# Normalization of the attention output through the z gates' buffers, its loads begun by ScalarE, and a fixed order up to the third feed-forward pair

## The chip, the cores and the metric

The kernel runs on one core of one Trainium2 chip. The metric is device time in microseconds (us) of one execution. Names of engines are those of the profile: PE is TensorE's matmul, DVE is VectorE, ACT is ScalarE, POOL is GpSimd, SP is SyncE, which here only issues transfers (its queue is SPq in the profile). ACT issues transfers too, in order with its other instructions.

## The reference

One hybrid decoder layer of width 1024 on 1024 positions, in float32. Cut to what matters:

```python
h = rms_norm(x, norm_mix_g)
z, xbc, dt_raw, q_a, kv_a, k_rope_raw, gates = split(h @ w_in)
y_ssd = ssd_mixer(z, xbc, dt_raw, ...) @ w_ssd_proj
y_mla = mla_mixer(q_a, kv_a, k_rope_raw, ...) @ w_mla_proj
g_ssd, g_mla = split(sigmoid(gates + gate_b), 2)
x = x + (g_ssd * y_ssd + g_mla * y_mla) @ w_o
h = rms_norm(x, norm_ffn_g)
u = causal_depthwise_conv(h @ w_up, conv_ffn_w, conv_ffn_b)      # 3 taps, 2 * 2816 channels
u_gate, u_val = split(u, 2)
x = x + (silu(u_gate) * u_val) @ w_down
```

`ssd_mixer` puts `xbc` through a causal convolution and silu, runs a state-space scan in chunks of 128 positions over 4 groups of 8 heads, multiplies by silu(z) and normalizes by group. `mla_mixer` is causal softmax attention with 16 heads of 64 values.

## The kernel before

**Products.** Every float32 operand of a large product is split into a high and a low part of a reduced float32 type (fp32r): ACT casts the high part (L127), and DVE or POOL subtracts to get the low part (L128). A product is three matmuls for each 128 x 128 x 512 piece (L149, L150, L151: high by high, high by low, low by high). A tile of weights for 128 output rows comes as two raw transfers of 256 KB (`wraw`, L134, two buffers), issued from SP; ACT casts `whi`, and POOL makes `wlo` until the last state-space group, DVE after it. Activations are held split in tiles `h`; `load_act` (L156) and `load_at` (L256) load a raw tile and split it.

**Stages.** In the profile's time: the norm and the small projections until about 100 us; attention until about 706 us, with gate tiles (`gate_tile`) and z tiles (`z_tiles`) as background work on PE; the last of these z tiles until about 750 us; the six tiles of the first convolution group (`conv_group(0)`: the B and C rows of the group, then four x tiles) until about 842 us; state-space groups 0 to 2 until about 1180 us, with the next convolution group and z tiles as background; group 3 with the attention output's projection (`mla_tiles`) in the background until about 1345 us; the projections by `w_ssd` and `w_o`; the seam, in which the first three pairs of feed-forward tiles (`q0`, `q1`, `q2`) begin, until about 1690 us; the steady pairs until about 2050 us; the product by `w_down`.

**What lies in memory between stages.** Attention writes its unnormalized output to `at_d` and 1/l, the reciprocal of each softmax denominator, to `l_d`. `normalize(n)` (L926), called sixteen times from the state-space loop (L874 and what follows), makes it whole: it loads a 128 x 512 piece of `at_d` into a tile `rb` (L934), broadcasts two rows of `l_d` into a second tile `rb` (L936, two transfers), multiplies on POOL (L937), and at the next call stores the piece back (L929). All of it is issued from SP. `load_at` reads the finished pieces, eight in `z_tiles(14, 15)` into tiles `rb` and eight in `mla_tiles` into tiles `lt`. The z tiles go to `z_d`, 256 KB each; `z_load` (L749) brings 256 KB of them per chunk into a tile `zt` (issued from ACT), and DVE uses it at L862. `abc_load` (L741) broadcasts 512 KB per chunk, also from ACT. In `mla_tiles`, `one` (L944) loads a gate tile of `g_d` into a tile `rb` (L947), combines it with the product and stores it to `m_d` (L954).

**What sets the order.** PE's instructions are always in the order of the program. For the other engines a scheduler chooses the order from what each instruction needs, buffers among it: the sixteen normalizations are called once per chunk of groups 0 and 1, but their data is there earlier, and nothing but their buffers holds them. Buffers are taken in turn by name within a pool; the pool `dp` (L734) has two of each name unless `bufs` says otherwise, so before there were three `rb`, shared by both tiles of `normalize`, `load_at` and `one`, and two `zt`. Between `strict` (L1267) and `strict_end` (L1355) each engine except SP keeps the order of the program by added dependencies; this covers part of the seam.

**The feed-forward pairs.** A pair is a gate tile and a value tile of 1024 positions. Each is computed by a scheme of seven products p1 to p7 on sums of blocks of the operands. For one pair: `w_raw` loads, `w_first`, `w_sums`, `w_second`, `w_third`, `w_fourth` make and split the weight sums; `p5`, `p6`, `p7`, `p3`, `p4` are products on PE; `both_sums` (L1221, the sum at L1223) reads the accumulator that `p3` goes on to; `c22` (L1233, the sum at L1235) reads the one that `p4` goes on to; `c11`, `c21` and `p3`'s last line write the other quarters of the rows `ug` and `uv`. `gate` (L1250) convolves `ug` (one ACT step, two DVE steps at L1243) and applies silu; `value` (L1260) convolves `uv`, multiplies with the gate (L1262) and stores.

Of the kernel before, what the change touches and what calls it, by code (L numbers as in the profile page):

```python
# [9 lines left out]
F32 = mybir.dt.float32  # L10
F32R = mybir.dt.float32r
I32 = mybir.dt.int32
AF = mybir.ActivationFunctionType
# [4 lines left out]
P = 128  # L18
# [9 lines left out]
FFT = 22  # L28
# [44 lines left out]
def tile_hybrid_layer(ctx: ExitStack, tc: tile.TileContext, x, cols, cons, w_main, w_small, w_uq, w_ukv,  # L73
# [180 lines left out]
    at = []  # L254

    def load_at(k, s, pool, name):  # L256
        raw = pool.tile([P, 512], F32, name=name, bufs=3)
        nc.sync.dma_start(out=raw, in_=at_d[k * P:(k + 1) * P, s])
        t = act_tile()
        split(raw, t[:, 0, :], t[:, 1, :])  # L260
        return t
# [472 lines left out]
    with tc.tile_pool(name="dp", bufs=2) as dp, tc.tile_pool(name="psx", bufs=1, space=PSUM) as psx, \  # L734
# [14 lines left out]
        def z_load(n):  # L749

            if n < GROUPS * NT:
                g, c = divmod(n, NT)
                t = dp.tile([P, 4, P], F32, name="zt")
                nc.scalar.dma_start(out=t, in_=z_d[4 * g * P:4 * (g + 1) * P, c * P:(c + 1) * P]
                                    .rearrange("(j p) t -> p j t", p=P))
                zts.append(t)
# [169 lines left out]
        def normalize(n):  # L926

            if stores:
                nc.sync.dma_start(out=stores[0][0], in_=stores[0][1])  # L929
                stores.pop()  # L930
            if n < 16:
                k, s = n // 2, hs_(n % 2)
                raw, rb = [dp.tile([P, 512], F32, name="rb", bufs=3) for _ in range(2)]
                nc.sync.dma_start(out=raw, in_=at_d[k * P:(k + 1) * P, s])  # L934
                for hd in range(2):
                    nc.sync.dma_start(out=rb[64 * hd:64 * hd + 64, :], in_=l_d[2 * k + hd, s].partition_broadcast(64))  # L936
                G.tensor_tensor(raw, raw, rb, op=ALU.mult)  # L937
                stores.append((at_d[k * P:(k + 1) * P, s], raw))

        def mla_tiles():  # L940

            at1 = []

            def one(w, ct, half):  # L944
                s = hs_(half)
                gt = dp.tile([P, 512], F32, name="rb", bufs=3)
                nc.sync.dma_start(out=gt, in_=g_d[(8 + ct) * P:(9 + ct) * P, s])  # L947
                ps = lin_tile()
                for k, _ in enumerate(steps([w], (at, at1)[half], ps, range(KD), KD)):
                    if len(at1) < 8 and k % 4 == 0:  # L950
                        at1.append(load_at(len(at1), hs_(1), lt, "lt"))
                    yield True
                V.scalar_tensor_tensor(gt, gt, 1.0, ps, op0=ALU.add, op1=ALU.mult)
                nc.sync.dma_start(out=m_d[ct * P:(ct + 1) * P, s], in_=gt)  # L954

            for ct in range(4):
                yield from one(load_w(w_mla[ct], [P, KD, P]), ct, 0)
            for ct in range(4, 8):
                w = load_w(w_mla[ct], [P, KD, P])
                for half in range(2):  # L960
                    yield from one(w, ct, half)
            for ct in range(4):
                yield from one(load_w(w_mla[ct], [P, KD, P]), ct, 1)
                ya0[ct] = load_act(y_d, ct * P, hs_(0))
# [63 lines left out]
    def w_raw(q):  # L1028
        q.r1 = up.tile([P, KD, P], F32, name="ur1", bufs=2)
        q.r2 = up.tile([P, KD, P], F32, name="ur2", bufs=2)  # L1030
        nc.sync.dma_start(out=q.r1, in_=w_up[q.j])
        nc.sync.dma_start(out=q.r2, in_=w_up[FFT + q.j])
# [14 lines left out]
    def w_first(q):  # L1047
        q.a = w_split(q.r1, w_tiles(0), G)
# [14 lines left out]
    def w_fourth(q, n=3):  # L1063
        q.d = w_split(q.r1[:, 4:8, :], w_tiles(n, n == 1), V)
# [8 lines left out]
    with tc.tile_pool(name="ep", bufs=2) as ep:  # L1073
# [127 lines left out]
        def gate_row(q):  # L1201
            q.ug = up.tile([P, T + 2], F32, name="ug", bufs=2)
            G.memset(q.ug[:, 0:2], 0.0)

        def c11(q):
            s1 = lt.tile([P, 512], F32, name="lt")
            S.copy(s1, q.x)
            V.tensor_tensor(q.ug[:, 2:514], q.y, s1, op=ALU.add)

        def p5(q):  # L1210
            q.z = bank6()
            drain([product(q.z, q.b, 0, "t1", True, True)])
# [16 lines left out]
        def value_row(q):  # L1229
            q.uv = ux[0].tile([P, T + 2], F32, name="uv", bufs=2)  # L1230
            G.memset(q.uv[:, 0:2], 0.0)
# [5 lines left out]
        def conv(q, kind, u):  # L1237
            c = ux[0].tile([P, T], F32, name=f"uc{kind}", bufs=2 - kind)
            ct = kind * FFT + q.j
            cw = CG_FW + 3 * ct  # L1240
            S.activation(c, u[:, 2:T + 2], AF.Identity, bias=col(CG_FB + ct), scale=col(cw + 2))
            for k in range(2):
                V.scalar_tensor_tensor(c, u[:, k:k + T], col(cw + k), c, op0=ALU.mult, op1=ALU.add)  # L1243
            return c

        def p3(q):
            drain([product(q.z, q.d, 0, "22", False, True)])
            V.tensor_tensor(q.ug[:, 514:1026], q.z, q.s2, op=ALU.add)

        def gate(q):  # L1250
            q.gate = conv(q, 0, q.ug)
            S.activation(q.gate, q.gate, AF.Silu)

        def p4(q):
            drain([product(q.y, q.e or q.c, 0 if q.e else 4, "t4", False, True)])
# [1 line left out]
        def c21(q):  # L1257
            V.tensor_tensor(q.uv[:, 2:514], q.y, q.s2, op=ALU.add)  # L1258

        def value(q):  # L1260
            c = conv(q, 1, q.uv)
            V.tensor_tensor(q.gate, q.gate, c, op=ALU.mult)  # L1262
            nc.sync.dma_start(out=a_d[q.j * P:(q.j + 1) * P, :], in_=q.gate)

# [85 lines left out]
    for n, q in enumerate((q0, q1)):  # L1352
        w_fourth(q, 3 if n == 0 else 1)
        p4(q)
    strict_end = len(nc.cur_bb.bb.instructions)  # L1355
    w_raw(q2)
    w_sums(q2)
    for q in (q0, q1):
        value_row(q)
        S.copy(q.uv[:, 514:1026], q.q)  # L1360
        c21(q)
    w_second(q2, V)
    w_third(q2)
    p3(q0)
    gate(q0)
    p3(q1)
    w_fourth(q2)
    q = q2

    rows = "p a b -> p (a b)"  # L1370
# [6 lines left out]
        split(raw, *first[k])  # L1377

    for j in range(3, FFT + 1):
        nx = None  # L1380
        if j < FFT:
            nx = Pair()
            nx.j = j
            w_raw(nx)
            w_first(nx)
        p5(q)
        if j == 3:
            gate_row(q)
            c11(q)
        if nx:  # L1390
            w_sums(nx)
        p6(q)
        if j == 3:

            value(q0)
            gate(q1)
        if nx:
            gate_row(nx)
        if nx:
            w_second(nx)  # L1400
        if not nx:
            for k in range(2):
                first_acts(k)
        p7(q)
        c22(q)
        p3(q)
        if j == 3:
            value(q1)
        gate(q)
        if nx:  # L1410
            w_fourth(nx)
        p4(q)
        c21(q)
        if not nx:
            for k in range(2, 4):
                first_acts(k)
        value(q)
        if nx:
            w_third(nx)
            drain([p12(nx)])  # L1420
            c11(nx)
        q = nx
# [130 lines left out]
```

## Time and profile before

| | us |
|---|---|
| median of 3 executions | 2294.0 |
| their lowest and highest | 2285.99, 2294.86 |
| the profiled execution, whole | 2296.51 |
| its span, first to last instruction | 2294.4 |
| mean granted TensorE clock in it | 0.988 |

Durations come from that one profiled execution. A row of a group names the line, the engine, the operation, what it writes and reads, and how often. In a row of waits, what stands left of the arrow sat idle until what stands right of it was done. A row of windows gives, for a stretch of the span, its length, the busy time of each engine with the number of instructions, the granted TensorE clock as a share of full speed, the share of time in which the transfer engines were busy, and GB/s.

### The profile page before, as it was taken

To read this page: it belongs to the slowest core of one execution; us is meant where nothing else is said; L and a number is where in the kernel's file an instruction comes from. 1 tells how busy PE (TensorE), PEld (TensorE's weight loads), DVE (VectorE), ACT (ScalarE), POOL (GpSimd) and SP (SyncE) were. 2 spreads that over 40 slices of the span, in tenths; PEclk is the share of its full clock that TensorE was granted. 3 is DMA by queue.
4 is the path that set the end of the run, shared out by engine and by line. 5 is a ranking of instruction groups with operands and counts; after the bars stand their busy time and mean duration, and the time that the engine had idled before them with its cause. 6 is when DMAs were issued, how large, how long until landed. Compare 5 with 4: busy or idle time off the path is not lost. (4 is left out here: it accounts for less than half of the span.)

```text
span 2294.4 us, 31427 instructions
## 1 busy us (share of the span) xinstructions
PE 2205.7 (96%) x11488; PEld 1769.3 (77%) x11488; DVE 1430.9 (62%) x2496; ACT 1014.1 (44%) x1852; POOL 755.5 (33%) x821
## 2 busy tenths in 40 slices
PE   8999999999998879999998999999989999999999
PEld 7877777777776667777876778989778888888887
DVE  4566565667662348887876755645887767774432
ACT  5454454454543226565654423424544444443221
POOL 2244432444333444343423310003175555510000
PEclk9999999999999999999999999999999999999999
DMA  3111111111113542545356685543122222227541
GB/s 141 57 66 48 48 42 52 53 48 41 54 48 117 168 147 75 126 104 124 97 156 189 170 280 197 178 144 116 55 92 83 83 83 83 83 101 269 189 148 65
DMA packets 158906, 253.57 MB, mean 111 GB/s; under 512 B 13504, under 2 KB 68480, under 8 KB 158752
## 3 DMA queue, kind: packets, MB, share of 16 engines
q1 hardware_dynamic: 101232, 214.73, 27.2%
q10 hardware_dynamic: 57520, 36.84, 6.8%
q8 instruction: 90, 1.47, 0.3%
q14 instruction: 64, 0.52, 0.1%
HBM read 194.63 MB, written 56.89 MB: 110 GB/s over the span
## 5 line engine op out<-in xcount | busy, mean ns | idle before, releaser
L149 PE MATMUL lin<-h,whi 128*128 128x512 f32 x1440 | 601.1, 417 | 16.4 <-ACT whi L127 10.5
L151 PE MATMUL lin<-h,wlo 128*128 128x512 f32 x1440 | 570.2, 396 | 16.9 <-POOL wlo L128 15.9
L150 PE MATMUL lin<-h,whi 128*128 128x512 f32 x1440 | 568.2, 395 | 0.0
L149 PEld LDWEIGHTS lin<-h,whi 128*128 128x128 f32 x1440 | 274.3, 191 | 124.0 <-issue 57.0
L151 PEld LDWEIGHTS lin<-h,wlo 128*128 128x128 f32 x1440 | 273.5, 190 | 83.6 <-POOL wlo L128 21.3
L150 PEld LDWEIGHTS lin<-h,whi 128*128 128x128 f32 x1440 | 274.7, 191 | 53.7 <-issue 7.3
L127 ACT CAST whi<-wraw 128x512 fp32r<-128x512 f32 x276 | 165.3, 618 | 301.9 <-PE lin L150 118.0
L128 POOL TENSOR_TENSOR wlo<-wraw,whi 128x512 fp32r<-128x512 f32 x134 | 198.8, 1498 | 188.6 <-ACT whi L127 188.5
L621 ACT ACTIVATE e<-s 128x512 f32<-128x512 f32 (+1 forms) x192 | 93.5, 491 | 162.1 <-DVE s L619 111.2
L128 DVE TENSOR_TENSOR wlo<-wraw,whi 128x512 fp32r<-128x512 f32 x142 | 99.7, 721 | 93.2 <-ACT whi L127 93.1
L626 POOL TENSOR_TENSOR acc<-acc,e 128x512 f32<-128x512 f32 (+3 forms) x80 | 79.2, 990 | 224.1 <-ACT acc L624 134.4
L128 DVE TENSOR_TENSOR h<-ar,h 128x1024 fp32r<-128x1024 f32 x40 | 48.7, 1225 | 109.0 <-ACT h L127 108.9
L808 ACT ACTIVATE seg<-abc,acum 128x128 f32<-128x128 f32 x256 | 82.2, 390 | 41.8 <-PE yp L849 35.2
L127 ACT CAST h<-ar 128x1024 fp32r<-128x1024 f32 x40 | 42.0, 1054 | 125.8 <-PE lin L150 115.0
L770 DVE SCALAR_TENSOR_TENSOR xg<-craw,cl,xg 128x1024 f32<-128x1024 f32 x48 | 76.6, 1596 | 33.3 <-ACT xg L768 31.5
L149 PE MATMUL dps<-whi,h 128*128 128x512 f32 x240 | 93.4, 389 | 0.0
L150 PE MATMUL dps<-wlo,h 128*128 128x512 f32 x240 | 93.4, 389 | 0.0
L151 PE MATMUL dps<-whi,h 128*128 128x512 f32 x240 | 93.4, 389 | 0.0
L626 DVE TENSOR_TENSOR acc<-acc,e 128x512 f32<-128x512 f32 (+3 forms) x80 | 58.4, 730 | 48.9 <-ACT e L621 33.2
L632 PE MATMUL pv<-e,vt 128*64 128x512 f32 (+3 forms) x384 | 83.1, 513 | 0.0
L1096 POOL TENSOR_TENSOR h<-x,h 128x512 fp32r<-128x512 f32 x8 | 11.1, 1390 | 214.9 <-ACT h L1095 214.9
L1043 ACT CAST xhi<-ur 128x512 fp32r<-128x512 f32 (+1 forms) x41 | 34.0, 830 | 91.7 <-PE dps L150 86.6
(566 smaller groups left out, 5157.9 us busy)
## 6 DMA issues: line engine op xcount, KB each, us to landing
wraw<-in_w_main SPq DMA_DIRECT2D x112, 256.0 KB
ur<-in_w_up SPq DMA_DIRECT2D x44, 512.0 KB
ar<-a_d SPq DMA_DIRECT2D x40, 512.0 KB
abc<-ac_d ACTq DMA_DIRECT2D x32, 512.0 KB
wraw<-in_w_ssd SPq DMA_DIRECT2D x64, 256.0 KB
wraw<-in_w_down SPq DMA_DIRECT2D x44, 256.0 KB
a_d<-uc SPq DMA_DIRECT2D x22, 512.0 KB
g_d<-lt SPq DMA_DIRECT2D x32, 256.0 KB
```

The costliest lines, as they stand in the source:

```text
L127: S.copy(hi, raw)
L128: (eng or V).tensor_sub(lo, raw, hi.bitcast(F32))
L149: PE.matmul(ps, lhsT=ah, rhs=bh, start=first, stop=False, **more)
L150: PE.matmul(ps, lhsT=ah, rhs=bl, start=False, stop=False, **more)
L151: PE.matmul(ps, lhsT=al, rhs=bh, start=False, stop=last, **more)
L621: S.activation(e[:, c0:512], ps[:, 0:w], AF.Exp)
L626: (V if hd else G).tensor_tensor(accs[hd][:, c0:512], accs[hd][:, c0:512], e[:, c0:512], op=ALU.add)
L632: PE.matmul(pv[hd * 64:(hd + 1) * 64, c0:512], lhsT=vt[:, j, hd * 64:(hd + 1) * 64], rhs=es[hd][:, c0:512], start=first, stop=last)
L770: V.scalar_tensor_tensor(c, raw[:, k:k + T], col(cw + k), c, op0=ALU.mult, op1=ALU.add)
L808: S.activation(seg[:, hd, :], abc[:, hd, :], AF.Relu, bias=acum[:, c, 8 * g + hd:8 * g + hd + 1], scale=-1.0)
L1043: S.copy(hi, r)
L1096: eng.tensor_sub(lo, v, hi.bitcast(F32))
```

## The change

It has four parts.

1. In `normalize` the broadcast of 1/l goes into a tile `zt`, shared with the z gates' loads; `zt` has three buffers instead of two, and `rb` two instead of three. The three `zt` buffers are taken in turn by z loads and broadcasts, so a broadcast waits for the use of an earlier z tile, and a z load for an earlier normalizing product.
2. `load_at` issues its sixteen transfers from ACT instead of SP. Its tiles `rb` have two buffers; `lt` keeps the pool's three.
3. `one` in `mla_tiles` has its gate tiles in two buffers `rb` instead of three.
4. In the seam `gate` and `value` can be called in two parts (convolution; silu or product and store), the fixed order reaches to the second part of `value(q1)`, behind `p3(q2)`, and the steps of the third pair and the beginning of the fourth are written out in it. The loop over pairs then begins with what is left of the third pair.

The diff, cut to its core:

```diff
--- before.py
+++ after.py
@@ -254,8 +254,8 @@
     at = []
     def load_at(k, s, pool, name):
-        raw = pool.tile([P, 512], F32, name=name, bufs=3)
-        nc.sync.dma_start(out=raw, in_=at_d[k * P:(k + 1) * P, s])
+        raw = pool.tile([P, 512], F32, name=name)
+        nc.scalar.dma_start(out=raw, in_=at_d[k * P:(k + 1) * P, s])
         t = act_tile()
         split(raw, t[:, 0, :], t[:, 1, :])
         return t
@@ -750,7 +750,7 @@
             if n < GROUPS * NT:
                 g, c = divmod(n, NT)
-                t = dp.tile([P, 4, P], F32, name="zt")
+                t = dp.tile([P, 4, P], F32, name="zt", bufs=3)
                 nc.scalar.dma_start(out=t, in_=z_d[4 * g * P:4 * (g + 1) * P, c * P:(c + 1) * P]
                                     .rearrange("(j p) t -> p j t", p=P))
                 zts.append(t)
@@ -930,7 +930,9 @@
                 stores.pop()
             if n < 16:
                 k, s = n // 2, hs_(n % 2)
-                raw, rb = [dp.tile([P, 512], F32, name="rb", bufs=3) for _ in range(2)]
+                raw = dp.tile([P, 512], F32, name="rb")
+
+                rb = dp.tile([P, 4, P], F32, name="zt", bufs=3).rearrange("p a b -> p (a b)")
                 nc.sync.dma_start(out=raw, in_=at_d[k * P:(k + 1) * P, s])
                 for hd in range(2):
                     nc.sync.dma_start(out=rb[64 * hd:64 * hd + 64, :], in_=l_d[2 * k + hd, s].partition_broadcast(64))
@@ -943,7 +945,7 @@
             def one(w, ct, half):
                 s = hs_(half)
-                gt = dp.tile([P, 512], F32, name="rb", bufs=3)
+                gt = dp.tile([P, 512], F32, name="rb")
                 nc.sync.dma_start(out=gt, in_=g_d[(8 + ct) * P:(9 + ct) * P, s])
                 ps = lin_tile()
                 for k, _ in enumerate(steps([w], (at, at1)[half], ps, range(KD), KD)):
@@ -1247,9 +1249,11 @@
             drain([product(q.z, q.d, 0, "22", False, True)])
             V.tensor_tensor(q.ug[:, 514:1026], q.z, q.s2, op=ALU.add)
-        def gate(q):
-            q.gate = conv(q, 0, q.ug)
-            S.activation(q.gate, q.gate, AF.Silu)
+        def gate(q, part=None):
+            if part != 1:
+                q.gate = conv(q, 0, q.ug)
+            if part != 0:
+                S.activation(q.gate, q.gate, AF.Silu)
         def p4(q):
             drain([product(q.y, q.e or q.c, 0 if q.e else 4, "t4", False, True)])
@@ -1257,10 +1261,12 @@
         def c21(q):
             V.tensor_tensor(q.uv[:, 2:514], q.y, q.s2, op=ALU.add)
-        def value(q):
-            c = conv(q, 1, q.uv)
-            V.tensor_tensor(q.gate, q.gate, c, op=ALU.mult)
-            nc.sync.dma_start(out=a_d[q.j * P:(q.j + 1) * P, :], in_=q.gate)
+        def value(q, part=None):
+            if part != 1:
+                q.value = conv(q, 1, q.uv)
+            if part != 0:
+                V.tensor_tensor(q.gate, q.gate, q.value, op=ALU.mult)
+                nc.sync.dma_start(out=a_d[q.j * P:(q.j + 1) * P, :], in_=q.gate)
@@ -1352,19 +1358,41 @@
     for n, q in enumerate((q0, q1)):
         w_fourth(q, 3 if n == 0 else 1)
         p4(q)
-    strict_end = len(nc.cur_bb.bb.instructions)
+    for q in (q0, q1):
+        value_row(q)
+    for q in (q0, q1):
+        S.copy(q.uv[:, 514:1026], q.q)
+        c21(q)
     w_raw(q2)
     w_sums(q2)
-    for q in (q0, q1):
-        value_row(q)
-        S.copy(q.uv[:, 514:1026], q.q)
-        c21(q)
+    value(q0, 0)
+    p3(q0)
     w_second(q2, V)
     w_third(q2)
-    p3(q0)
-    gate(q0)
     p3(q1)
+    p5(q2)
+    gate(q0, 0)
+    gate_row(q2)
+    c11(q2)
     w_fourth(q2)
+    p6(q2)
+    gate(q0, 1)
+    value(q0, 1)
+    gate(q1, 0)
+    nx = Pair()
+    nx.j = 3
+    w_raw(nx)
+    w_first(nx)
+    w_sums(nx)
+    p7(q2)
+    c22(q2)
+    value(q1, 0)
+    gate(q1, 1)
+    p3(q2)
+    value(q1, 1)
+    strict_end = len(nc.cur_bb.bb.instructions)
+    gate_row(nx)
+    w_second(nx)
     q = q2
     rows = "p a b -> p (a b)"
@@ -1377,35 +1405,26 @@
         split(raw, *first[k])
     for j in range(3, FFT + 1):
-        nx = None
-        if j < FFT:
-            nx = Pair()
-            nx.j = j
-            w_raw(nx)
-            w_first(nx)
-        p5(q)
-        if j == 3:
-            gate_row(q)
-            c11(q)
-        if nx:
-            w_sums(nx)
-        p6(q)
-        if j == 3:
-
-            value(q0)
-            gate(q1)
-        if nx:
-            gate_row(nx)
-        if nx:
-            w_second(nx)
-        if not nx:
-            for k in range(2):
-                first_acts(k)
-        p7(q)
-        c22(q)
-        p3(q)
-        if j == 3:
-            value(q1)
+        if j > 3:
+            nx = None
+            if j < FFT:
+                nx = Pair()
+                nx.j = j
+                w_raw(nx)
+                w_first(nx)
+                gate_row(nx)
+            p5(q)
+            if nx:
+                w_sums(nx)
+            p6(q)
+            if nx:
+                w_second(nx)
+            else:
+                for k in range(2):
+                    first_acts(k)
+            p7(q)
+            c22(q)
+            p3(q)
         gate(q)
         if nx:
             w_fourth(nx)
```

What this moves. On SP, in the stretch that feeds the last z tiles and the first convolution group. Before (`wraw` is a raw weight tile; `rb`, `at_d` and `l_d` as above):

```order
L929 DMA at_d<-rb 128x512
L936 DMA rb<-l_d 64x512 x2
L934 DMA rb<-at_d 128x512
L134 DMA wraw<-in_w_main 128x512
L929 DMA at_d<-rb 128x512
L134 DMA wraw<-in_w_main 128x512
L936 DMA rb<-l_d 64x512 x2
L934 DMA rb<-at_d 128x512
L929 DMA at_d<-rb 128x512
L936 DMA rb<-l_d 64x512 x2
L934 DMA rb<-at_d 128x512
```

The same stretch of SP in the changed kernel (line numbers are shifted by two from here on):

```order
L929 DMA at_d<-rb 128x512
L936 DMA rb<-at_d 128x512
L134 DMA wraw<-in_w_main 128x512
L296 DMA z_d<-lt 128x512
L134 DMA wraw<-in_w_main 128x512 x13
L296 DMA z_d<-lt 128x512
L134 DMA wraw<-in_w_main 128x512 x2
L296 DMA z_d<-lt 128x512
L938 DMA zt<-l_d 64x512 x2
L929 DMA at_d<-rb 128x512
L134 DMA wraw<-in_w_main 128x512 x2
L936 DMA rb<-at_d 128x512
```

Two normalizations are issued ahead of this stretch and the pieces of two more loaded; the other fourteen come after the thirteen weight transfers, one for every one or two pairs of weight transfers.

On ACT, where the loads of `at_d` are cast (h<-rb) while group 3 begins. Before, these loads are SP's:

```order
L127 CAST h<-rb 128x512
L754 DMA zt<-z_d 128x4x128
L127 CAST h<-rb 128x512
L293 ACTIVATE lt<-lin 128x512
L127 CAST h<-rb 128x512
L808 ACTIVATE seg<-abc,acum 128x128
L746 DMA abc<-ac_d 128x8x128
L127 CAST h<-rb 128x512
```

In the changed kernel:

```order
L127 CAST h<-rb 128x512
L258 DMA rb<-at_d 128x512
L293 ACTIVATE lt<-lin 128x512
L127 CAST h<-rb 128x512
L258 DMA rb<-at_d 128x512 x2
L808 ACTIVATE seg<-abc,acum 128x128
L746 DMA abc<-ac_d 128x8x128
L127 CAST h<-rb 128x512 x2
L293 ACTIVATE lt<-lin 128x512
L870 ACTIVATE sq__11464<-xg 128x512
L754 DMA zt<-z_d 128x4x128
L258 DMA rb<-at_d 128x512 x2
```

Each load is now issued one to three casts ahead of its own, and shares ACT's queue with the broadcasts (abc) and the z loads.

On DVE in the seam, around the sum at L1223 (`both_sums` of the third pair; `uc` is a convolution's result, L1262 the product of gate and value, L1235 `c22`). Before:

```order
L1208 TENSOR_TENSOR ug<-dps,lt 128x512
L1243 SCALAR_TENSOR_TENSOR uc_15902<-ug,cl,uc_15902 128x1024
L1262 TENSOR_TENSOR uc_15827<-uc_15827,uc_15896 128x1024
L1223 TENSOR_TENSOR lt<-dps,lt 128x512
L1243 SCALAR_TENSOR_TENSOR uc_15902<-ug,cl,uc_15902 128x1024
L1235 TENSOR_TENSOR uv<-dps,lt 128x512
```

In the changed kernel, where the same sums stand at L1225 and L1237, the convolution's steps at L1245 and the product at L1268:

```order
L1210 TENSOR_TENSOR ug<-dps,lt 128x512
L1046 TENSOR_TENSOR xlo_15867<-ur_15797,xhi_15866 128x512
L1225 TENSOR_TENSOR lt<-dps,lt 128x512
L1268 TENSOR_TENSOR uc_15857<-uc_15857,uc_15806 128x1024
L1245 SCALAR_TENSOR_TENSOR uc_15889<-ug,cl,uc_15889 128x1024 x2
L1237 TENSOR_TENSOR uv<-dps,lt 128x512
```

The sum of `both_sums` has moved ahead of a convolution step and of the product; between it and `c22` stand now the product and two steps.

## The prediction

> **What bounds the kernel now.** I read the head of the page first, then a table of windows by stage, and then the waits inside the windows that lose time.
>
> ```profile
> span 2294.4 us, 31427 instructions
> PE 2205.7 (96%) x11488; PEld 1769.3 (77%) x11488; DVE 1430.9 (62%) x2496; ACT 1014.1 (44%) x1852; POOL 755.5 (33%) x821
> ...
> core 0: us, PE busy (x) PEld busy (x) DVE busy (x) ACT busy (x) POOL busy (x), PEclk, DMA share, GB/s
> 700.00:750.00 50.00, 43.84 (x200) 33.73 (x199) 7.85 (x14) 16.67 (x37) 8.99 (x11) 0.97 0.46 136
> 750.00:800.00 50.00, 43.24 (x173) 34.16 (x172) 19.53 (x12) 12.73 (x18) 24.86 (x16) 0.93 0.51 162
> 800.00:850.00 50.00, 36.46 (x147) 28.50 (x147) 25.98 (x19) 14.27 (x19) 25.01 (x18) 0.92 0.46 152
> 900.00:1180.00 280.00, 275.81 (x1715) 221.50 (x1713) 240.00 (x373) 169.54 (x317) 111.78 (x103) 1.00 0.43 113
> 1180.00:1300.00 120.00, 104.68 (x584) 81.50 (x579) 73.41 (x137) 54.81 (x114) 40.04 (x38) 0.93 0.64 174
> 1600.00:1690.00 90.00, 79.16 (x386) 65.02 (x385) 75.74 (x101) 50.01 (x76) 27.77 (x20) 0.96 0.20 73
> 1690.00:2050.00 360.00, 360.00 (x1569) 294.38 (x1568) 264.32 (x232) 156.22 (x173) 195.46 (x141) 1.00 0.24 84
> ```
>
> PE is the bound, 96% of the span, and its order is the same before and after. So the change can only give or take PE's idle time, and the slow matmuls at a lower granted clock that follow idle time. The table says where these are. From 700 to 850 us (the last z tiles and the first convolution group) PE is idle 150 − 43.84 − 43.24 − 36.46 = 26.5 us, and the clock of 0.97, 0.93 and 0.92 costs another 0.03·43.84 + 0.07·43.24 + 0.08·36.46 = 7.3 us: **33.8 us lost**. The state-space groups (900 to 1180) lose 4.2 us, the attention projection (1180 to 1300) 15.3 us and 0.07·104.68 = 7.3 us of clock, the seam before the feed-forward pairs (1600 to 1690) 10.8 us and 0.04·79.16 = 3.2 us. The steady pairs lose nothing.
>
> What PE, ACT, POOL and SP's queue wait for from 715 to 870 us (us in total, times, longest), and the 16 normalizing products (ns min/median/max, first and last start):
>
> ```profile
> PE lin L151 <- POOL wlo L128: 15.2, 8, 3.2
> PE lin L149 <- DVE lt L294: 5.9, 2, 3.2
> PE xp L798 <- DVE xg L775: 5.3, 1, 5.3
> ACT whi L127 <- DMA wraw<-in_w_main: 40.4, 12, 13.5
> POOL rb L937 <- DMA rb<-l_d: 57.3, 13, 15.5
> SPq L929 <- POOL rb L937: 33.1, 10, 7.8
> SPq L934 <- DMA at_d<-rb: 11.2, 10, 4.4
> ...
> L937 POOL TENSOR_TENSOR rb<-rb x16: 1263/1442/2325, 733.5 to 843.9; 128x512 f32<-128x512 f32 x16
> ```
>
> PE waits for POOL's low halves of weights; ACT, which makes the high halves, waits 40.4 us for the raw weights; and they come late because SP, which issues them in order, stands 33.1 us at stores (L929) that wait for POOL's normalizing product, and 11.2 us at loads that wait for a store to land. POOL itself stands 57.3 us in front of L937. All 16 normalizations lie between 733.5 and 843.9 us, inside the lossy windows.
>
> **The change, part by part.**
>
> *Normalization paced by the z gates' buffers.* Two of the sixteen products stay early. The other fourteen, with their two broadcast loads and store each, leave SP's and POOL's queues of the convolution group; thirteen weight loads now follow one another. Not all of the 33.8 us is theirs: PE's wait of 3.2 us on L294 at the first product is behind ACT, and I count 3 us as staying. The remaining 30.8 us over 16 normalizations is 1.9 us each; two stay, so the gain is 14 · 1.9 = **27 us**. The bounds are 15.2 us (only the waits on POOL's halves) and 33.8 us (everything).
>
> The fourteen then stand in the state-space groups, one a chunk, each with two broadcast loads, a product and a store, and a z load on ACT that waits for that product. What they meet there:
>
> ```profile
> SPq L134 <- POOL wlo L128: 184.2, 36, 18.5
> ...
> POOL wlo L128 <- ACT whi L127: 50.9, 22, 4.4
> ...
> ACT whi L127 <- DMA wraw<-in_w_main: 8.7, 3, 3.9
> ```
>
> From 900 to 1180 us SP waits 184.2 us for a buffer to put raw weights in (5.1 us at a time), so loads are early there, not late; ACT waits only 8.7 us for them, and POOL is busy 111.8 of 280 us. A product of 1.4 us with up to 4.4 us (57.3/13) of wait for its broadcast in front has that cover. If the cover is gone, each costs PE what it did before, 1.9 us; so the cost lies between nothing and 14 · 1.9 = 27 us. Nothing can be won from the move itself in a stage that loses 4.2 us. I take **+4 us**, near the row that says SP is early. The z load on ACT has three buffers where it had two, but shares them with the broadcasts in turn; its product is due more than a chunk ahead, so I add nothing for it.
>
> One row bears on POOL beside VectorE: L937 takes 1263 ns at least and 2325 ns at most, and DVE is busy 240 of 280 us. The Trainium skill, "SBUF — State Buffer", section "SBUF: two separate sides", says that GpSimd and a VectorE operation with two SBUF inputs exclude each other for a whole instruction. The rows do not separate an exclusive lock from a slowdown of both. By the rule this part can cost VectorE time even with POOL idle, which is a rival below.
>
> *Loads of the normalized attention issued from ACT, and the gate tiles in two buffers.* These act from 1180 to 1300 us:
>
> ```profile
> PE lin L149 <- ACT whi L127: 7.1, 2, 5.8
> ACT whi L127 <- DMA wraw<-in_w_mla: 24.3, 8, 6.2
> ACT h L127 <- DMA lt<-at_d: 13.1, 3, 9.1
> ACT h L127 <- DMA rb<-at_d: 8.6, 4, 4.9
> SPq L947 <- DMA m_d<-rb: 39.1, 8, 9.5
> ```
>
> Sixteen loads of 256 KB leave SP's queue, where weights queue behind them (24.3 us of ACT's waits are for those weights), and enter ACT's, where they queue behind the broadcasts of 512 KB (abc) and the z loads, and where the cast of each follows close on its load. ACT gains on weights and loses on these. With two buffers for the gate tiles SP's load waits for the store of two tiles earlier instead of three; the longest such wait was 9.5 us, and it already stands ahead of weight loads. The bounds are −14 us (7.1 us of PE's waits on ACT gone, with the 7.3 us of clock) and +22 us: the seven waits of 21.7 us were 3.1 us each, and if fourteen loads wait so it is 43.4 us, 21.7 more. Since ACT is busy only 54.81 of 120 us and one side offsets the other, I take **0**.
>
> ACT's 24.3 us of waits on weights are waits in SP's line, with the DMA share at 0.64. The Trainium skill, "DMA: Bandwidth & Descriptors", section "Issuing engines are not separate DMA queues", says that all issuers share the same 16 engines and that a second issuer saves only issue time. By that rule this part gives nothing, which is the 0 taken; the row speaks of a line of blocked instructions, which the rule does not cover and which could give up to the 14.
>
> *The seam.* PE's waits from 1600 to 1690 us, and VectorE's instructions around the longest (start, duration):
>
> ```profile
> PE dps L149 <- DVE lt L1223: 6.4, 1, 6.4
> PE dps L149 <- DVE ug L1342: 2.1, 1, 2.1
> ...
> 1670.43 0.68 DVE L1208 TENSOR_TENSOR ug<-dps,lt 128x512 f32<-128x512 f32 x1
> 1671.03 2.77 DVE L1243 SCALAR_TENSOR_TENSOR uc<-ug,cl,uc 128x1024 f32<-128x1024 f32 x1
> 1673.73 2.28 DVE L1262 TENSOR_TENSOR uc<-uc,uc 128x1024 f32<-128x1024 f32 x1
> 1675.93 0.68 DVE L1223 TENSOR_TENSOR lt<-dps,lt 128x512 f32<-128x512 f32 x1
> 1676.53 2.78 DVE L1243 SCALAR_TENSOR_TENSOR uc<-ug,cl,uc 128x1024 f32<-128x1024 f32 x1
> 1679.23 0.68 DVE L1235 TENSOR_TENSOR uv<-dps,lt 128x512 f32<-128x512 f32 x1
> ...
> 1676.66 0.79 PE L149 MATMUL dps<-h,xhi 128*128 128x512 f32 x1 [6.42 <-DVE lt L1223]
> ```
>
> PE waits for the sum at L1223, which stands behind a convolution step and a product of gate and value. The fixed order puts these two behind the sum: it comes 2.77 + 2.28 = 5.1 us earlier, at about 1670.9. But the next result that PE needs, the sum at L1235, now has the product and two convolution steps in front: 1670.9 + 0.6 + 2.2 + 2.8 + 2.8 = 1679.3 (each step at the 2.8 of the two in the rows), no earlier than the 1679.23 of before. PE's twelve matmuls of the product took until about 1682 at half clock; started 5 us sooner, they end near 1677 and PE waits for that sum until about 1680. What stays is about 2 us of 5, and with less slow clock behind a shorter gap I take **−3 us**. The bounds are 0 (it all moves to L1235) and −6.4 − 3.2 = −10 us (the wait and the clock both go). The raw loads and splits of the fourth pair become fixed as well; they feed pairs that lose nothing in the steady windows, and I count them as nothing.
>
> *Sum.* −27 + 4 + 0 − 3 = −26 us against the profiled execution's 2296.5 us (span 2294.4), so 2270.5. That execution lay 2.5 us above the median of the runs shown, 2294.0; against the median the forecast is **2268 us**.
>
> **The rivals.**
>
> 1. *The stalls move with the normalizations.* The product stands in POOL's order ahead of weight splits, its store in SP's ahead of weight loads, exactly as before, only in another stage. Price 14 · 1.9 = 27 us in full instead of 4: 2268 + 23 = **2291 us**, no change. For it speaks the 4.4 us wait in front of each product; against it the 184.2 us for which SP waits for buffers there.
> 2. *VectorE becomes late in the state-space groups.* Each product beside VectorE costs what L937's spread shows, 2325 − 1263 = 1.06 us, in a stage where DVE is busy 86%: 14 · 1.06 = 15 us, of which 4 are in the sum already: 2268 + 11 = **2279 us**. The 40 us of DVE's idle time there speak against it.
> 3. *The projection gains too*, since weights no longer stand behind sixteen loads: all 14 us of the lower bound, **2254 us**.
> 4. *The other side: ACT becomes the bound in the projection.* Its casts stand right behind loads that stand behind 512 KB broadcasts on its own queue. Had each of the fourteen loads the longest wait shown, 9.1 us, it would be 127 us of waits in a stage where ACT has 120 − 54.81 = 65 us free: 62 us longer, **2330 us**. It decides from the point where the excess passes the 26 us won: (65 + 26)/14 = 6.5 us a load, about twice the mean of 3.1 us.
> 5. *The change doesn't do what it says*: excluded for the main part, since SP's rows show the thirteen loads in a row.
>
> **How the numbers follow.** Forecast 2268 us, by itself 2258 to 2276: 0.60. Rival 1: 0.15. Rival 2: 0.09. Rival 3: 0.10. Rival 4: 0.06. The range takes in rivals 1, 2 and 3 and the 6.6 us that the main gain's upper bound adds: 2250 to 2291, with rival 4 and the upper half of rival 1 outside, about 0.15. A measurement here tells about 0.5%, 11.5 us, from no change; faster means below 2282.5. The forecast and rivals 2 and 3 are faster, 0.79 together; rival 1 is the same, 0.15; rival 4 is slower, 0.06.
>
> **What the profile of after would show.** Right: from 715 to 850 us ACT's wait for raw main weights falls from 40.4 to below 12 us, POOL's wait in front of the product from 57.3 to some 10 us, and the three windows together have PE busy above 140 us at a clock near 1; the products run from 733 us until after 1050 us. From 900 to 1180 us PE's idle time stays below 10 us; above 20 is rival 1, and DVE named as its releaser is rival 2. From 1180 to 1300 us ACT's waits for at_d stay below 45 us; above 90 is rival 4. In the seam the wait at L1223 is gone and a shorter one on L1235 has come. The prediction fails if the weights stay late in the convolution group for another reason: then ACT still waits some 30 us for raw weights with the normalizations gone.

## The result and the profile after

| | before | changed |
|---|---|---|
| median of 5 executions, us | 2287.65 | 2309.89 |
| lowest to highest, us | 2285.99 to 2294.86 | 2303.7 to 2313.51 |
| ratio to before, 95% interval | 1 | **1.0083** (1.0059 to 1.0108) |
| span of the profiled execution, us | 2294.4 | 2306.3 |

The changed kernel is slower by 0.83%: some 19 us between the means, 22 us between the medians. The forecast was 2268 us, 26 us faster than the 2294.0 known then. The profiled execution of before lay 9 us above its median of five and that of after 2 us below, so the spans differ by 12 us only.

The head of the page and a table of windows of the changed kernel (columns as in the prediction):

```profile
span 2306.3 us, 31442 instructions
PE 2208.7 (96%) x11488; PEld 1772.7 (77%) x11488; DVE 1410.3 (61%) x2496; ACT 1013.9 (44%) x1852; POOL 743.0 (32%) x821
...
700.00:750.00 50.00, 42.30 (x201) 33.02 (x199) 7.04 (x13) 15.33 (x35) 8.91 (x11) 0.99 0.45 138
750.00:800.00 50.00, 48.51 (x205) 39.97 (x206) 21.75 (x17) 19.19 (x28) 12.99 (x13) 0.94 0.26 76
800.00:850.00 50.00, 50.00 (x262) 40.35 (x261) 29.94 (x33) 20.08 (x35) 18.08 (x16) 1.00 0.21 64
850.00:1050.00 200.00, 176.51 (x1043) 139.58 (x1042) 147.07 (x235) 106.03 (x203) 86.39 (x78) 0.94 0.58 141
1180.00:1300.00 120.00, 101.19 (x559) 78.40 (x556) 66.62 (x126) 48.91 (x102) 38.33 (x35) 0.90 0.63 175
```

From 700 to 850 us PE has lost most of its idle time, as forecast: it is busy 140.81 of these 150 us instead of 123.54. But from 850 to 1050 us, where PE was busy 195.81 us before at a clock of 0.99, it is now busy 176.51 at 0.94. That window of before:

```profile
850.00:1050.00 200.00, 195.81 (x1193) 155.74 (x1192) 168.18 (x255) 118.99 (x226) 80.06 (x74) 0.99 0.40 107
```

PE executes the same 11,488 matmuls in the same order in all kernels here (the names of the other kernels are explained below). So the start of a matmul in one trace minus the start of the same matmul in the trace of before says how far ahead (negative) or behind PE is at that place. At six places, by the time of before, for all runs:

| us ahead (−) or behind | 725 | 850 | 1125 | 1300 | 1600 | 1725 |
|---|---|---|---|---|---|---|
| changed kernel | −0.1 | −25.7 | 0.4 | 6.0 | 7.4 | 11.5 |
| e1_seam | 0.0 | −4.0 | −4.6 | −8.0 | −6.3 | 0.0 |
| e2_noseam | −1.5 | −25.6 | 0.8 | 5.8 | 6.9 | 6.8 |
| e3_zsp | −1.5 | −25.3 | −11.1 | −12.4 | −11.1 | −9.9 |
| e4_zt5 | −1.2 | −24.3 | −6.4 | 0.8 | 0.6 | 0.2 |
| e5_rb3 | −0.8 | −27.6 | −1.4 | −1.5 | −1.3 | −1.8 |
| e6_atact | 0.4 | 2.3 | 2.8 | 1.1 | 1.1 | 1.7 |
| e7_zsp_rb3 | −3.0 | −28.5 | −16.1 | −27.2 | −25.6 | −25.4 |
| e8_pace | 0.7 | −24.3 | −1.4 | −6.7 | −6.4 | −2.6 |
| e9_late | −1.1 | −36.4 | −24.2 | −23.7 | −23.6 | −23.8 |
| e10_zsp_late | −0.5 | −32.7 | −22.2 | −32.6 | −29.0 | −28.9 |
| e11_before_zsp | 0.1 | −1.0 | −2.3 | 0.3 | 1.6 | 1.2 |
| e12_pace_late | 1.6 | −33.9 | −24.2 | −29.0 | −28.9 | −26.7 |

The changed kernel wins 25.7 us by 850, gives back 26.1 by 1125, and loses 5.6 in the projection and 4.1 in the seam. One caution: e1_seam has the code of before up to 1600 us and yet differs by up to 8 us there, so one trace tells a stage's difference no finer than that; smaller claims rest on the ratios.

**Where the gain went.** What ACT and POOL waited for in the groups, from 850 to 1060 and from 840 to 1060 us of the changed kernel:

```profile
ACT craw L766 <- POOL rb L939: 19.4, 2, 13.4
ACT whi L127 <- POOL rb L939: 16.6, 2, 10.4
ACT seg L808 <- POOL rb L939: 5.1, 2, 4.4
...
POOL rb L939 <- DMA zt<-l_d: 51.4, 11, 13.5
```

No arithmetic in these rows needs POOL's normalizing product (L939) directly. What does is the z load, which ACT issues and which takes over the product's buffer. One such stand (an engine held at one instruction, with all that follows on it), from the timelines of SP, POOL, ACT and PE (start, duration, engine):

```profile
951.55 4.91 SPq L938 DMA_DIRECT2D zt<-l_d  x2
962.22 1.26 POOL L939 TENSOR_TENSOR rb<-rb,zt 128x512 f32<-128x512 f32 x1 [13.48 <-DMA zt<-l_d]
949.97 0.59 ACT L835 COPY st<-sn 128x512 f32<-128x512 f32 x1
963.51 0.43 ACTq L754 DMA_DIRECT2D zt<-z_d  x1
963.98 0.59 ACT L766 COPY craw<-lin 128x512 f32<-128x512 f32 x1 [13.42 <-POOL rb L939]
...
964.62 0.79 PE L149 MATMUL lin<-h,whi 128*128 128x512 f32 x1 [7.43 <-ACT craw L766]
```

ACT is done at 950.56 and next in its order is the z load. It stands until the product has ended at 963.48; the product stood 13.48 us for its broadcast, which SP finished issuing at 956.46. Behind ACT's z load waits the copy that empties PE's accumulator (L766), so PE stops for 7.43 us, and its next matmuls take 0.79 and 0.63 us instead of the 0.39 before the gap. DVE uses the z tile only at 996.37, 33 us after its issue.

PE's longest wait in the groups besides this one names DVE, but ends the same way. Followed back through the timelines of POOL, ACT, DVE and PE:

```profile
1024.43 1.28 POOL L939 TENSOR_TENSOR rb<-rb,zt 128x512 f32<-128x512 f32 x1 [9.44 <-DMA zt<-l_d]
1025.74 0.43 ACTq L754 DMA_DIRECT2D zt<-z_d  x1
1026.20 0.62 ACT L127 CAST whi<-wraw 128x512 fp32r<-128x512 f32 x1 [10.45 <-POOL rb L939]
1027.73 1.24 ACT L768 ACTIVATE xg<-craw,cl 128x1024 f32<-128x1024 f32 x1
1029.00 1.47 DVE L770 SCALAR_TENSOR_TENSOR xg<-craw,cl,xg 128x1024 f32<-128x1024 f32 x1 [9.49 <-ACT xg L768]
1032.29 2.05 PE L908 MATMUL np__10011<-cn,grr 128*128 128x128 f32 x8 [7.17 <-DVE grr L124]
```

DVE is late here because it sat idle for 9.49 us until ACT had left its z load; the step that PE waits for (L124, at 1031.99) stands behind L770 in DVE's order. The first stand of this kind lies before 850 us, at the last z tiles, and PE's wait of 7.83 us there has the same source (through ACT's copy at 750.13 and DVE's step L294 at 750.75, both behind the cast shown):

```profile
749.14 0.43 ACTq L754 DMA_DIRECT2D zt<-z_d  x1
749.61 0.62 ACT L127 CAST whi<-wraw 128x512 fp32r<-128x512 f32 x1 [12.01 <-POOL rb L939]
751.49 0.80 PE L149 MATMUL lin<-h,whi 128*128 128x512 f32 x1 [7.83 <-DVE lt L294]
```

**The projection and the seam.** PE's waits in the whole span:

```profile
PE lin L149 <- DVE rb L955: 9.7, 1, 9.7
...
PE dps L149 <- DVE lt L1225: 5.9, 1, 5.9
...
PE dps L149 <- DVE uv L1237: 3.8, 1, 3.8
```

The first, in the projection:

```profile
1275.41 0.33 SPq L949 DMA_DIRECT2D rb<-g_d  x1
1275.83 0.38 SPq L956 DMA_DIRECT2D m_d<-rb  x1
1284.57 0.69 DVE L955 SCALAR_TENSOR_TENSOR rb<-rb,lin 128x512 f32<-128x512 f32 x1 [11.05 <-DMA rb<-g_d]
1285.11 0.32 SPq L949 DMA_DIRECT2D rb<-g_d  x1
1285.31 0.79 PE L149 MATMUL lin<-h,whi 128*128 128x512 f32 x1 [9.73 <-DVE rb L955]
```

The gate tile of 1275.41 takes over the buffer of two tiles earlier, and SP held its issue until that tile's store, issued at 1266.43, had landed:

```profile
SPq L949 <- DMA m_d<-rb: 7.1, 1, 7.1
```

DVE can use the tile only at 1284.57, 9.2 us after its issue; until then the accumulator stays full. Why the tile took that long to land was not tested. In the seam, DVE's sums that PE waits for, first in the changed kernel and then, for the fourth pair, before:

```profile
1676.09 0.68 DVE L1225 TENSOR_TENSOR lt<-dps,lt 128x512 f32<-128x512 f32 x1
1683.44 0.68 DVE L1237 TENSOR_TENSOR uv<-dps,lt 128x512 f32<-128x512 f32 x1
1707.65 0.68 DVE L1225 TENSOR_TENSOR lt<-dps,lt 128x512 f32<-128x512 f32 x1
```

```profile
1697.64 0.68 DVE L1223 TENSOR_TENSOR lt<-dps,lt 128x512 f32<-128x512 f32 x1
```

The third pair's sum comes no later than before (1676.09 against 1675.93) although PE entered the seam 7.4 us later. But the wait on c22 is there, and the fourth pair's sum comes 31.6 us after the third's instead of 21.7: the 5.9 us at L1225 are for this one.

### The profile page after: what moved, and what is told of

It is laid out like the page before. It is cut to its first block, busy times and chain, and to the rows that moved or that the text cites. A ratio compares the mean times of both kernels' runs of the same rounds, so it can differ in the third digit from the quotient of the medians.

```text
span 2306.3 us, 31442 instructions
## 1 busy us (share of the span) xinstructions
PE 2208.7 (96%) x11488; PEld 1772.7 (77%) x11488; DVE 1410.3 (61%) x2496; ACT 1013.9 (44%) x1852; POOL 743.0 (32%) x821
## 4 chain that ended last, share of the span: by engine, by line
PE 67%; DVE 12%; DMA 10%; ACT 5%; issue 3%; POOL 2%; SPq 0%; ACTq 0%; POOLq 0%; DVEq 0%
PE lin L149 10%; PE lin L151 10%; PE lin L150 10%; PE dps L149 7%; PE dps L151 7%; PE dps L150 7%; PE pv L632 2%; DMA wraw<-in_w_ssd 2%; DMA zt<-l_d 2%; PE s L149 2%; PE s L151 1%; PE s L150 1%; DMA m_d<-rb 1%; PE s L589 1%; DMA wraw<-in_w_mla 1%
## 5 line engine op out<-in xcount | busy, mean ns | idle before, releaser
L128 POOL TENSOR_TENSOR wlo<-wraw,whi 128x512 fp32r<-128x512 f32 x134 | 191.2, 1442 | 171.4 <-ACT whi L127 163.8
L770 DVE SCALAR_TENSOR_TENSOR xg<-craw,cl,xg 128x1024 f32<-128x1024 f32 x48 | 67.3, 1403 | 40.7 <-ACT xg L768 38.1
L1098 POOL TENSOR_TENSOR h<-x,h 128x512 fp32r<-128x512 f32 x8 | 11.1, 1392 | 216.5 <-ACT h L1097 216.5
L1045 ACT CAST xhi<-ur 128x512 fp32r<-128x512 f32 (+1 forms) x41 | 33.9, 830 | 97.2 <-PE dps L150 80.4
```

The lines of the kernel that those rows point to most:

```text
L128: (eng or V).tensor_sub(lo, raw, hi.bitcast(F32))
L770: V.scalar_tensor_tensor(c, raw[:, k:k + T], col(cw + k), c, op0=ALU.mult, op1=ALU.add)
L1045: S.copy(hi, r)
```

## The experiments

Ratios are to the kernel before, run on the same chip, with 95% intervals.

**e1_seam and e2_noseam: the seam alone, and everything but the seam.** e1_seam is the kernel before with the hunks on `gate`, `value`, `strict_end` and the loop over pairs; e2_noseam has all the others.

> The kernel before with the fourth part of the change alone (fixed order in the seam). Theory S: the wait in front of the third pair's sum goes (6.8 us), but a wait for c22 (about 4 us) and one for the fourth pair's sum (about 6 to 7 us) come, so it ends 3 to 5 us later than before, ratio 1.001 to 1.002. Rival: the two new waits in the changed kernel come from the seam being entered 7 us later; then it ends 2 to 4 us earlier, ratio 0.998 to 0.999. The PE waits of the seam tell which.

> The changed kernel without its fourth part (seam as before). Theory S: 3 to 5 us faster than the changed kernel, 14 to 19 us slower than before, ratio about 1.006. Rival: 2 to 4 us slower than the changed kernel, ratio about 1.010. All stages up to 1600 us as in the changed kernel by both: about 25 us won by 850 us and all of it given back by 1050 us.

Measured: e1_seam 1.0016 (1.0000 to 1.0033), e2_noseam 1.0058 (1.0039 to 1.0076). PE's waits in the seam of e1_seam:

```profile
PE dps L149 <- DVE lt L1223: 5.8, 1, 5.8
PE dps L149 <- DVE uv L1235: 3.8, 1, 3.8
```

Both new waits are there although this run entered the seam 6.3 us early, so they are not a matter of when it is entered; it lost those 6.3 us there. By the ratios the fixed order costs about 4 us (e1_seam) or 6 (the changed kernel against e2_noseam), though one interval touches 1 and the other overlaps that of the changed kernel. The main loss is elsewhere: e2_noseam wins 25.6 us by 850 and has given all of it back by 1125.

**e3_zsp: the z loads issued from SP.**

```diff
 # z_load, on e2_noseam
-nc.scalar.dma_start(out=t, in_=z_d...)
+nc.sync.dma_start(out=t, in_=z_d...)
```

> As e2_noseam, with the z loads issued from SP instead of ACT. Theory A: ACT's stand at the z load, behind a normalizing product, is what gives the gain back from 875 to 1051 us. Then the 58 us of ACT's waits for the product vanish, PE loses under 8 us there instead of 27, and the kernel is about 20 us faster than e2_noseam, 2265 to 2275 us, ratio 0.990 to 0.995. Rival B: the normalizations carry their stalls with them on POOL and SP (product ahead of weight splits, store ahead of weight loads). Then the 27 us stay or grow, since SP now stands at one more wait: ratio 1.005 to 1.012.

Measured: 0.9989 (0.9977 to 1.0002), 16 us faster than e2_noseam. ACT no longer waits for the product, but POOL still stands in front of it (e3_zsp, the product's line):

```profile
its engine sat idle before it (us, times) until:
  DMA zt<-l_d: 71.2, 13
```

PE gives back 14.2 us from 850 to 1125 instead of 26.4. Theory A was right in direction and explains about half; the expected 2265 to 2275 us were missed (the median is 2286.69), and for the other half rival B's mechanism, POOL's stand in front of the product, is left.

**e4_zt5: five buffers.**

```diff
-name="zt", bufs=3
+name="zt", bufs=5
-name="xde")   -name="bt")
+name="xde", bufs=1)   +name="bt", bufs=1)
```

> As e2_noseam, with five buffers zt instead of three (room made by one buffer instead of two for xde and bt, whose readers are done before the next write). A z load then waits for the product two chunks back, and still stands on ACT. Theory A: ACT's waits for the product fall under 8 us, PE's loss from 875 to 1051 us under 8 us. Four normalizations instead of two are early, so some 22 us are won up to 850 us: 2268 to 2278 us, ratio 0.991 to 0.996. Rival B: the products and stores stand in POOL's and SP's queues as before, so the loss stays at 20 us or more: ratio 1.003 to 1.008.

Measured: 1.0029 (1.0016 to 1.0042). It fits neither cleanly: ACT's waits for the product fell to 10.0 us from 840 to 1060, not under 8, while PE gave back 17.9 us, since POOL and SP still stand (ACT's longest waits for the product, 26.4 us in two, now lie before 840), and the 10 us wait at L955 came again (10.3). It beats e2_noseam by 7 us.

**e5_rb3, e6_atact, e8_pace: the buffers `rb` and the loads of `at_d`.** e5_rb3 gives `rb` three buffers again (on e2_noseam) and, as e4_zt5, takes one from `xde` and `bt`; so do the kernels built on it, e7, e9, e10 and e12. e6_atact has only the issuer of the second part of the change, with three buffers; e8_pace is e2_noseam with those loads back on SP.

```diff
 # e5_rb3: load_at, normalize, one             # e6_atact, on before         # e8_pace, on e2_noseam
-name="rb")                                    -nc.sync.dma_start(out=raw    -nc.scalar.dma_start(out=raw
+name="rb", bufs=3)                            +nc.scalar.dma_start(out=raw  +nc.sync.dma_start(out=raw
```

> As e2_noseam, with three buffers rb as before for the raw pieces, load_at and the gate tiles (room made by one buffer instead of two for xde and bt). Theory C: the 9.5 us for which PE waits at L955 comes from the gate tiles' two buffers, whose load waits for the store of two tiles earlier to land. Then that wait goes, the stage from 1180 to 1300 us wins 2 to 6 us instead of losing 5, and the ratio is 1.001 to 1.004. Rival: the wait comes from the loads on ACT or from the phase in which the stage is entered; then a wait of that size stays and the ratio is 1.005 to 1.007. The groups before 1180 us as in e2_noseam by both.

> The kernel before with load_at's sixteen loads issued from ACT and nothing else. Theory D: they leave SP's queue to the weights, ACT's 24 us of waits for weights from 1180 to 1300 us fall by half and PE wins 2 to 6 us: ratio 0.997 to 0.999. The forecast's view (both sides offset): ratio 0.999 to 1.001. Rival: behind the broadcasts on ACT's queue they stop ACT longer than the weights did; PE loses 3 us or more, ratio 1.001 to 1.004.

> As e2_noseam, with load_at's loads issued from SP as before, so that only the pacing and the two buffers rb are left of the change. Theory D (loads on ACT help in the projection): 2 to 6 us slower than e2_noseam, ratio 1.007 to 1.009. Rival (they hurt): 2 us or more faster, ratio 1.002 to 1.005. The groups up to 1180 us as in e2_noseam by both: about 25 us won by 850 us, given back by 1050 us.

Measured: e5_rb3 1.0020 (1.0008 to 1.0032), e6_atact 1.0017 (0.9995 to 1.0038), e8_pace 1.0025 (1.0010 to 1.0040). PE's longest waits from 1180 to 1320 us in e5_rb3:

```profile
PE lin L149 <- ACT whi L127: 8.0, 2, 4.6
PE np__12351 L908 <- DVE grr L124: 4.7, 1, 4.7
```

The wait at L955 is gone, and e5_rb3 is 9 us faster than e2_noseam. It is gone in e8_pace too, at two buffers, and also in e3_zsp. So in these traces, one of each kernel, two buffers are needed for it (of the kernels with three, e6_atact shows 2.0 us of it and the others none) but do not suffice: it is in the changed kernel, e2_noseam and e4_zt5, all of which have the loads of `at_d` and of z on ACT. Theory C was right on the wait and the ratio, but the stage did not win the 2 to 6 us that it expected in e5_rb3 (1.4 us ahead at 1125, 1.5 at 1300). Theory D fell: the loads on ACT alone gain nothing (e6_atact), and taking them back wins 8 us where `rb` has two buffers (e8_pace). The Trainium skill, "DMA: Bandwidth & Descriptors", section "Issuing engines are not separate DMA queues", says that transfers of all issuers run on the same 16 engines and that a second issuer saves only the time of issuing. e6_atact agrees with it at 1.0017; the 8 us of e8_pace are not of its kind, and which wait behind a load on ACT makes them was not taken apart.

**e7_zsp_rb3: e3_zsp and e5_rb3 together.**

> e3_zsp with three buffers rb. Theory C: the projection stage, where e3_zsp was even with before, wins 2 to 6 us: ratio 0.996 to 0.998. Rival (no wait at L955 in e3_zsp, so nothing to win): as e3_zsp, 0.998 to 1.000.

Measured: 0.9944 (0.9927 to 0.9962), more than either had: it wins 11 us in the projection. Why there, where e5_rb3 won nothing, was not taken apart.

**e9_late and e10_zsp_late: the product one call later.** The product moves to the next call of `normalize`, behind POOL's last instruction before it; the store follows it.

```diff
 def normalize(n):
     if stores:
+        raw, rb = stores[0][1:]
+        last = [i for i in nc.cur_bb.bb.instructions if i.engine == mybir.EngineType.Pool][-1]
+        G.tensor_tensor(raw, raw, rb, op=ALU.mult)
+        tc.add_manual_dep(nc.cur_bb.bb.instructions[-1], last.name, ...)
...
-        G.tensor_tensor(raw, raw, rb, op=ALU.mult)
-        stores.append((at_d[k * P:(k + 1) * P, s], raw))
+        stores.append((at_d[k * P:(k + 1) * P, s], raw, rb))
```

> As e5_rb3 (z loads on ACT), with each normalizing product put one call later, behind POOL's last instruction before that call, so that its broadcast was loaded a chunk earlier. Theory A: what cost the groups their 26 us is that a product follows its own broadcast at once, with POOL in front of it and ACT, at the z load, behind it. Then POOL's waits for the broadcast (82 us in e2_noseam) and ACT's for the product (58 us) fall under 10 us, PE loses under 8 us from 875 to 1051 us, ratio 0.990 to 0.995. Rival E: the transfers and the product's busy time beside VectorE cost it, wherever they stand; then the loss stays above 15 us and the ratio at 0.999 to 1.003.

> e7_zsp_rb3 with the products one call later, as in e9_late. Theory A: the 12 us that e7_zsp_rb3 still gave back between 850 and 1075 us were POOL's waits in front of the product, with weight splits behind; they fall to under 5 us: ratio 0.989 to 0.992. Rival E: they stay, ratio 0.993 to 0.996.

Measured: e9_late **0.9914** (0.9893 to 0.9935), e10_zsp_late **0.9884** (0.9855 to 0.9913), the fastest kernel of all at a median of 2262.59 us and just below the range expected for it. The product's line in e9_late, in which nothing is named before it:

```profile
L931 POOL TENSOR_TENSOR rb<-rb,zt x16: 1269/1296/2308, 812.3 to 1046.3; 128x512 f32<-128x512 f32 x16
its engine sat idle before it (us, times) until:
who waited for it (us, times):
  ACT seg L810: 8.4, 3
  ACT xg L768: 3.6, 1
```

```profile
700.00:850.00 150.00, 148.50 (x711) 119.31 (x712) 66.13 (x77) 63.31 (x111) 40.12 (x43) 1.00 0.32 96
850.00:1050.00 200.00, 190.50 (x1172) 152.04 (x1167) 173.39 (x251) 116.09 (x221) 106.94 (x87) 0.98 0.60 155
```

The same sixteen products, of about the same length, beside a busier VectorE (173.39 us against 147.07 in the changed kernel) and with the transfer engines as busy (0.60 against 0.58), now cost the groups up to 1050 us about 7 us (36.4 ahead at 850, 29.2 at 1050), where e5_rb3 loses 26. Another 5 us go by 1125, after the last product; why was not taken apart. ACT still waits 12.0 us for the products, where under 10 was expected. Before 850 us e9_late wins 9 us more than e5_rb3, because now no product lies in that stretch (the first starts at 812.3, about where its convolution group ends). e9_late against e5_rb3 differs in the products' place alone: 1.0020 to 0.9914, 24 us. Theory A in its wider form holds; rival E falls, since the loss is 12 us at most, not over 15.

e10_zsp_late is less clear in its trace. The expectation that the 12 us of e7_zsp_rb3 would fall to under 5 was missed: it still gives back 7.8 us by 1050 and 10.5 by 1125. By the ratios it is 0.60% faster than e7_zsp_rb3, with intervals that do not touch; the two traces end only 3.5 us apart (e10 wins 4 us before 850 and 2 in the groups, and some is given back later), and e7's profiled execution was the fastest of its four.

**e11_before_zsp and e12_pace_late: controls.** e11_before_zsp is the kernel before with e3_zsp's edit; e12_pace_late is e9_late with e8_pace's.

> A control: the kernel before with the z loads issued from SP and nothing else. Before, no z load waits for a product, so by theory A this changes nothing: ratio 0.998 to 1.002. Rival: z loads on ACT cost by themselves, and e3_zsp gained from that: 0.993 to 0.996.

> e9_late with load_at's loads on SP as before. Theory (the loads on ACT cost some 7 us in e2_noseam against e8_pace, because they meet gate tiles with two buffers): with three buffers they cost nothing, ratio as e9_late within 0.0015. Rival (they cost by standing on ACT): 4 to 8 us faster than e9_late.

Measured: e11_before_zsp 1.0021 (1.0006 to 1.0036): z loads on SP gain nothing by themselves (it is just above the expected range, on the other side from the rival), so e3_zsp's gain was ACT's stand. e12_pace_late 0.9909 (0.9892 to 0.9927), the same as e9_late: with three buffers the ratios show no difference by who issues the loads of `at_d`.

## Why the prediction was wrong

- **The convolution group: right, in part by luck.** 27 us were forecast; PE was 25.7 us ahead at 850. ACT's waits for raw main weights fell from 53.3 us in the whole span (40.4 of them from 715 to 870) to 8.2. But I counted 3 us of PE's waits as staying, and 9.2 stayed from 715 to 850, 7.8 of them behind the first stand at a z load; where no product is left in this stretch (e9_late) 36.4 us are won by 850, more than my upper bound of 33.8.
- **The state-space groups: the wrong step.** I took 4 us from a range of nothing to 27, "near the row that says SP is early", and wrote of the z load that "its product is due more than a chunk ahead, so I add nothing for it". That the data was not due was true and did not matter: the z load is issued in its place in ACT's order, and ACT stands there until the product is done (41.1 us in six waits from 850 to 1060), with casts and copies behind it. What was measured is 26.1 us, close to the upper bound. By the ratios, moving that stand to SP took away 0.69% (e2_noseam to e3_zsp), and moving the product away from its own broadcast another 0.60% from POOL's side (e7_zsp_rb3 to e10_zsp_late). The row of SP's 184.2 us shows slack for raw weights; it says nothing of the engines that stand after the weights have landed.
- **Rival 1** named the right price, place and half of the mechanism (POOL's stand in front of the product); I gave it 0.15. PE's idle time from 900 to 1180 us was 16.7 us, between my marks of 10 (right) and 20 (rival 1), with 0.04 of the clock lost beside it.
- **Rival 2** did not occur, although its sign did: DVE is named for 11.3 us of PE's waits there (7.2 and 4.1). In both DVE itself had waited for ACT behind a z load, as the rows above show for the longer one, and e9_late keeps the products beside a busier VectorE. The rule behind it (the Trainium skill, "SBUF — State Buffer", section "SBUF: two separate sides", by which GpSimd and a VectorE operation with two SBUF inputs exclude each other) was not tested by itself.
- **The projection: 0 taken, about +6 measured.** The bound held the wait I had named, for a store to land, but I left it on SP "ahead of weight loads"; with two buffers it came, at 7.1 us, between a gate tile and the accumulator it empties. The loads on ACT, my rival 4, did not make ACT the bound: its waits for `at_d` from 1180 to 1300 us were 23.3 us, and my mark for rival 4 was 90.
- **The seam: −3 taken, about +4 measured.** The step to c22 was right (3.8 us of wait there). I stopped at the third pair; with the convolution steps and products that the order puts behind its sum, the fourth pair's sum comes 31.6 us after it instead of 21.7.
- **Sum:** 1 us of error in the convolution group, 22 in the groups, 6 in the projection and 7 in the seam make 36 of the 37.5 us by which the profiled execution (2308.05 us) missed the working's 2270.5.

## What to carry to other kernels

Here a transfer that took over a buffer waited at its issue, and everything behind it on the issuing engine waited too (13.4 us in the stand shown), although the transferred data was needed only 33 us later; so ask of a new buffer dependency where the waiting instruction stands, not when its data is due. Pacing work by buffers also fixes how close its parts lie: a product that can start only once its own input has just been requested puts that latency in front of its engine each time (84.1 us before fourteen products here), and one step of delay (request now, use at the next call) took these waits away (none is left in e9_late). When a wait in a chain of sums is moved, follow the chain until the steady state, not just to the next sum.

## What the hardware showed that was not expected

Issuing one broadcast of 64 x 512 from SP took between 0.44 and 2.81 us in the changed kernel (ns min/median/max, from 725 to 1075 us):

```profile
L938 SPq DMA_DIRECT2D zt<-l_d x30: 444/588/2809, 741.9 to 1059.8; - x30
```

In the stand shown above the two issues took 4.91 us together, while ACT's queue was moving the 512 KB broadcast issued shortly before. That the one slowed the other was not tested.
